# Squares summed by TensorE at a sublayer's end, additions to x on VectorE, low parts of the next weights on GpSimd

## Chip, cores and metric

One core of a Trainium2 chip runs the whole program. Its engines are PE (TensorE), DVE (VectorE), ACT (ScalarE), POOL (GpSimd) and SP (SyncE, which issues the DMAs). The metric is the time on the device of one execution in microseconds, as the median of several runs.

## The reference

The input is x (512 tokens of width 1024, fp32). A first block has a hybrid mixer, a memory cross attention and a SwiGLU FFN, each with a norm before and a norm after it. A second block has two layers of FFN, mixer and FFN, whose norms are modulated by vectors that come out of products of a condition `c` with 144 blocks of `w_ada`. What matters here is the form of the first block's sublayers and of the norm that follows:

```python
def rms_norm(x, g):
    xf = x.astype(jnp.float32)
    y = xf * lax.rsqrt(jnp.mean(xf * xf, axis=-1, keepdims=True) + RMS_EPS)
    return (y * g.astype(jnp.float32)).astype(x.dtype)
...
def swiglu(h, w_gate_up, w_down):
    g, u = jnp.split(h @ w_gate_up, 2, axis=-1)
    return (jax.nn.silu(g) * u) @ w_down
...
        y = swiglu(rms_norm(x, pre_ffn_g[l]), w_gate_up[l], w_down[l])
        x = x + rms_norm(y, post_ffn_g[l])
```

## The kernel before

x is kept transposed, as eight tiles X[m] of 128 features by 512 tokens (m = 0 to 7). Every large product runs as three products in a reduced fp32 format, on high and low parts of both factors. `weights()` loads a weight block of 128x1024 (`wr`), ACT makes its high part (`wh`, L338) and DVE, or an engine `e`, the low part, the rest of the subtraction (`wl`, L340). Three raw blocks, six high and six low parts can be alive.

PE runs in an order that a small planner (`Flow`) writes down ahead: every stream of work yields pieces with their cost on PE, or a wait whose length comes from a table of delays (`T`), and the order in which pieces come up is PE's order, kept as it is. The orders of DVE, ACT, POOL and SP are made by the language's scheduler, from the program and the dependences. Every engine works strictly in its order.

A sublayer's last product is taken in two halves of 256 tokens (`slab4`, products into `slh`). `end_post` handles the ends of the first block's three sublayers. For each m the slab's result is added to y on DVE (`evac`, L566), ACT squares y (L487) and POOL adds the squares up (`square_sum`, L490). When a half is through, a stream `norm(hf)` starts: PE sums the squares over features by products with ones (`ms`, L464, in `cols`), DVE makes 1/sqrt in twelve small steps (`rs_m`, `rs_y`, `rs_w`, `rs_a`, L447 to L455), and PE broadcasts the result over the partitions (`bc`, L476, in `spread`). Then for each m DVE scales y (L576) and x takes it up (L578; even m on DVE, odd m on POOL). In two of the three ends, those after the mixer and after cross attention (`apart` given), the high and low parts of the next products are made from x at once and the norm over x is applied later. The end of the FFN has no `apart`: squares of x are summed again on POOL, PE sums them over features, and a second broadcast comes before the next FFN's inputs `hh` and `hl` can be made (`norm_half`, L515 to L528). That FFN begins with five weight blocks at once (`dense_t` with `ahead` = 5, products `mm`), first all of one half of the tokens, then the other.

`ada()` loads a modulation block by DMA and reduces it on DVE (L795), one each time that `weights()` pulls it while `calm`; `modulated(n)` pulls what is missing for sublayer n.

## Time and profile before

| | us |
|---|---|
| median of 3 runs | 2888.01 |
| the runs | 2886.16 to 2888.03 |
| profiled execution | 2887.57 |
| its span | 2885.5 |
| PE busy | 2784.1 (96% of the span) |
| DVE busy | 1534.0 (53%) |
| ACT busy | 1027.6 (36%) |
| POOL busy | 383.5 (13%) |

The span reaches from the first to the last instruction of the profiled execution; about 2 us lie around it. PE's share is an average over the whole program. Where PE is not full is seen from its waits and from windows of the span. All times within the span are counted from its start. The end of the first FFN, the one end without `apart`, lies at 831 to 896 us; the ends after the mixer and after cross attention lie at about 312 to 370 and 450 to 510 us.

### The profile page before, as it was taken

The numbers are of one execution on the slowest core, as the hardware profiler recorded it, in microseconds if no ns is written. First come the engines' busy times: TensorE is split into PE (matmuls) and PEld (weight loads), VectorE is DVE, ScalarE is ACT, GpSimd is POOL, SyncE is SP. The second block draws the span as 40 slices with busy tenths as digits, with TensorE's granted clock in tenths as the row PEclk, the third lists the DMA queues.
The fourth block names the chain that finished last, engine by engine and source line by source line (L and its number), as shares of the span: only waits on it lengthen the run. The fifth ranks groups of instructions, "written<-read, shape, count | busy, mean of one in ns | idle before, by whom it ended". The sixth has DMA issues, their size and how long they took to land. (4 is left out here: it accounts for less than half of the span.)

```text
span 2885.5 us, 36900 instructions
## 1 busy us (share of the span) xinstructions
PE 2784.1 (96%) x14492; PEld 2355.3 (82%) x14492; DVE 1534.0 (53%) x2931; ACT 1027.6 (36%) x1725; POOL 383.5 (13%) x376
## 2 busy tenths in 40 slices
PE   8999998999989999998799999999999988999999
PEld 7888878888878888887588888888888875888888
DVE  6465666645456444466766454463333667643333
ACT  4355444323233222245543222342222535432221
POOL 3010303101032000024310000110000232200000
PEclk9999999999998999999999999999999997999999
DMA  5322322555433555431115555353332321133322
GB/s 164 121 69 88 103 88 74 168 160 169 148 114 123 160 169 161 139 116 54 52 52 162 156 174 159 112 173 110 102 95 88 95 62 34 52 98 93 102 90 71
DMA packets 94606, 326.07 MB, mean 113 GB/s; under 512 B 11232, under 2 KB 15584, under 8 KB 94432
## 3 DMA queue, kind: packets, MB, share of 16 engines
q1 hardware_dynamic: 94288, 323.53, 36.4%
q8 instruction: 114, 1.87, 0.3%
q14 instruction: 60, 0.49, 0.1%
q10 hardware_dynamic: 144, 0.18, 0.0%
HBM read 321.37 MB, written 2.10 MB: 112 GB/s over the span
## 5 line engine op out<-in xcount | busy, mean ns | idle before, releaser
L338 ACT ACTIVATE wh<-wr 128x1024 fp32r<-128x1024 f32 x456 | 482.3, 1060 | 1273.0 <-PE mm L347 494.8
L346 PE MATMUL mm<-hh,wh 128*128 128x512 f32 (+1 forms) x2344 | 856.9, 366 | 7.3 <-ACT fqk L1352 2.4
L348 PE MATMUL mm<-hh,wl 128*128 128x512 f32 (+1 forms) x2344 | 852.4, 364 | 3.0 <-DVE wl L340 3.0
L347 PE MATMUL mm<-hl,wh 128*128 128x512 f32 (+1 forms) x2344 | 852.9, 364 | 1.7 <-DVE hl L500 1.6
L340 DVE TENSOR_TENSOR wl<-wr,wh 128x1024 fp32r<-128x1024 f32 x440 | 541.8, 1233 | 343.1 <-ACT wh L338 341.2
L346 PEld LDWEIGHTS mm<-hh,wh 128*128 128x128 f32 x2344 | 448.4, 191 | 76.6 <-ACT fqk L1352 3.3
L348 PEld LDWEIGHTS mm<-hh,wl 128*128 128x128 f32 x2344 | 448.4, 191 | 71.2 <-DVE wl L340 3.6
L347 PEld LDWEIGHTS mm<-hl,wh 128*128 128x128 f32 x2344 | 448.2, 191 | 69.6 <-DVE hl L500 2.0
L795 DVE CUSTOM_DVE_ANT_0 ada<-ada,c 128x1024 f32<-128x1024 f32 x144 | 180.4, 1253 | 314.4 <-DMA ada<-in_w_ada_dram 314.2
L346 PE MATMUL dn<-uh,wh 128*128 128x512 f32 x720 | 280.1, 389 | 0.0
L347 PE MATMUL dn<-ul,wh 128*128 128x512 f32 x720 | 280.1, 389 | 0.0
L348 PE MATMUL dn<-uh,wl 128*128 128x512 f32 x720 | 280.1, 389 | 0.0
L490 POOL TENSOR_TENSOR acc<-sq,sq 128x256 f32<-128x256 f32 (+1 forms) x34 | 38.3, 1129 | 1377.2 <-ACT sq L487 1377.2
L633 DVE TENSOR_TENSOR sg<-mm,sg 128x512 f32<-128x512 f32 x110 | 75.9, 690 | 181.8 <-PE mm L348 177.4
L346 PE MATMUL mmt<-wh,hh 128*128 128x512 f32 x352 | 147.1, 418 | 12.1 <-ACT wh L338 8.2
L348 PEld LDWEIGHTS dn<-uh,wl 128*128 128x128 f32 x720 | 135.1, 188 | 28.1
L346 PEld LDWEIGHTS dn<-uh,wh 128*128 128x128 f32 x720 | 135.1, 188 | 28.1
L347 PEld LDWEIGHTS dn<-ul,wh 128*128 128x128 f32 x720 | 135.1, 188 | 28.0
L347 PE MATMUL mmt<-wl,hh 128*128 128x512 f32 x352 | 141.3, 402 | 0.5 <-DVE wl L340 0.5
L348 PE MATMUL mmt<-wh,hl 128*128 128x512 f32 x352 | 141.4, 402 | 0.0
L490 POOL TENSOR_TENSOR acc<-acc,sq 128x256 f32<-128x256 f32 (+1 forms) x140 | 122.5, 875 | 72.5 <-ACT sq L487 57.3
L669 DVE SCALAR_TENSOR_TENSOR X<-dn,gate,X 128x512 f32<-128x512 f32 x64 | 48.0, 750 | 155.6 <-PE dn L348 155.6
(322 smaller groups left out, 3611.1 us busy)
## 6 DMA issues: line engine op xcount, KB each, us to landing
wr<-in_f_gu_dram SPq DMA_DIRECT2D x176, 512.0 KB, 3.6
ada<-in_w_ada_dram SPq DMA_DIRECT2D x144, 512.0 KB, 4.2
wr<-in_f_dn_dram SPq DMA_DIRECT2D x88, 512.0 KB, 3.5
wr<-in_w_gu_dram SPq DMA_DIRECT2D x44, 512.0 KB, 3.6
wr<-in_w_in_dram SPq DMA_DIRECT2D x28, 512.0 KB, 3.5
wr<-in_m_t_dram SPq DMA_DIRECT2D x24, 512.0 KB, 3.5
wr<-in_w_dn_dram SPq DMA_DIRECT2D x22, 512.0 KB, 4.0
wr<-in_m_v_dram SPq DMA_DIRECT2D x16, 512.0 KB, 3.5
```

Source lines behind the costliest of these rows:

```text
L338: nc.scalar.activation(hi, raw, AF.Copy)
L340: (e or nc.vector).tensor_tensor(lo, raw, hi.bitcast(F32), op=OP.subtract)
L346: mm(ps, ah, bh, start=start, stop=False)
L347: mm(ps, ah, bl, start=False, stop=False)
L348: mm(ps, al, bh, start=False, stop=stop)
L490: nc.gpsimd.tensor_tensor(acc, accs.pop(), sq, op=OP.add)
L633: nc.vector.tensor_tensor(t, ps, t, op=OP.mult)
L669: self.nc.vector.scalar_tensor_tensor(self.X[m], ps, gate(m), self.X[m], op0=OP.mult, op1=OP.add)
L795: nc.vector.tensor_tensor_reduce(out=w, in0=w, in1=c, scale=1.0, scalar=0.0, op0=OP.mult, op1=OP.add, accum_out=ml[:, i:i + 1])
```

## The change

Four things change.

1. At all three ends of `end_post` only the squares of m = 0 to 5 are added up on POOL; those of m = 6 and 7 go to PE's sum as they are. A half's sum takes six products where the first half took two and the second four.
2. At the end without `apart`, the squares of x are not added up on POOL at all. Each goes to PE's sum as soon as the planner brings it up (`cols_of`), two products with one column each. The additions to x run on DVE except m = 1 and 4. The delay `squares` is gone.
3. In the FFN that follows this end, the five weight blocks taken at once get their low parts on POOL.
4. `ada` finishes a group in the step of its last block, and `modulated` remembers how far it is, so that it pulls no block more than it needs. 144 blocks remain; four of them (the 47th, 87th, 91st and 131st load) come later.

```diff
@@ weights
         if self.due >= 1.0:
             self.due -= 1.0
-            next(self.beside, None)
+            self.adas = next(self.beside, 6)
...
-    def dense_t(self, srcs, X, evac, ahead=0):
+    def dense_t(self, srcs, X, evac, ahead=0, e=None):
...
-            ws.append(self.weights(srcs[i]))
+            ws.append(self.weights(srcs[i], e))
...
+    def cols_of(self, tiles, scale, out):
+        ms, first = self.ps("x", "ms"), True
+        for sq in tiles:
+            if isinstance(sq, Wait):
+                yield sq
+                continue
+            for j in range(2):
+                self.nc.tensor.matmul(ms[:, j:j + 1], sq[:, j * 128:j * 128 + 128], self.ones1,
+                                      start=first, stop=True, skip_group_check=True)
+                first = False
+            yield 0.44
+        out.append(self.rsqrt(ms[:, :2], 2, scale, RMS_EPS))
+
-    def spread(self, accs, ncol, scale, out):
+    def spread(self, accs, ncol, scale, out, tiles=None):
         y = []
-        yield from self.cols(accs, ncol, scale, y)
+        yield from self.cols_of(tiles, scale, y) if tiles else self.cols(accs, ncol, scale, y)
...
@@ end_post
             nc.vector.tensor_tensor(y, ps, y, op=OP.add)
-            self.square_sum(sums, y, self.half, o == 0 or m % 4)
+            self.square_sum(sums, y, self.half, m < 6)
...
             yield from self.spread(accs, 2, 1.0 / D, bc)
-            for m in range(NK):
-                yield Wait(T["post"])
-                x, y = self.X[m][:, sl], Y[m][:, sl]
-                nc.vector.scalar_tensor_tensor(y, y, self.vec(gpost, m), bc[0], op0=OP.mult,
-                                               op1=OP.mult)
-                (nc.gpsimd if m % 2 else nc.vector).tensor_tensor(x, x, y, op=OP.add)
-                if apart:
-                    self.gain_half(hf, m, nxt[0], H)
-                else:
-                    self.square_sum(sums2, x, self.rot, m % 4)
+            def added():
+                for m in range(NK):
+                    yield Wait(T["post"])
+                    x, y = self.X[m][:, sl], Y[m][:, sl]
+                    nc.vector.scalar_tensor_tensor(y, y, self.vec(gpost, m), bc[0], op0=OP.mult,
+                                                   op1=OP.mult)
+                    e = nc.gpsimd if (m % 2 if apart else m in (1, 4)) else nc.vector
+                    e.tensor_tensor(x, x, y, op=OP.add)
+                    if apart:
+                        self.gain_half(hf, m, nxt[0], H)
+                    else:
+                        sq = self.half("sq")
+                        nc.scalar.activation(sq, x, AF.Square)
+                        yield sq
             if apart:
+                yield from added()
...
             else:
-                yield Wait(T["squares"])
-                bc = []
-                yield from self.spread(sums2, 2, 1.0 / D, bc)
-                yield from self.norm_half(hf, bc[0], nxt[0], nxt[1], H)
+                bc2 = []
+                yield from self.spread(None, 2, 1.0 / D, bc2, added())
+                yield from self.norm_half(hf, bc2[0], nxt[0], nxt[1], H)
...
@@ ada
-                    yield 3 * l + j
+                    if i % 24 < 23:
+                        yield 3 * l + j
...
+                yield 3 * l + j + 1
...
@@ modulated
-        while next(self.beside, 6) < n:
-            pass
+        while self.adas < n:
+            self.adas = next(self.beside, 6)
...
                 yield from self.ffn(I["f_gu"][2 * l + j // 2], I["f_dn"][2 * l + j // 2], H,
-                                    self.x_evac(g), end2)
+                                    self.x_evac(g), end2, self.nc.gpsimd if n == 3 else None)
```

The diff alone doesn't show where the scheduler and the planner put things. On PE, at the end of the first FFN, before: the rows from the end of the slab's second half (`slh`) to the first product of the next FFN (`mm`). `acc` are sums that POOL made, `sq` single squares, `rs_y` the end of an rsqrt chain.

```order
L348 MATMUL slh_7619<-uh_7265,wl_7310 128x256
L464 MATMUL ms_7694<-ones_78,acc_7540 128x1
L464 MATMUL ms_7694<-ones_78,acc_7645 128x1
L464 MATMUL ms_7694<-ones_78,acc_7540 128x1
L464 MATMUL ms_7694<-ones_78,acc_7645 128x1
L464 MATMUL ms_7714<-ones_78,acc_7609 128x1
L464 MATMUL ms_7714<-ones_78,acc_7692 128x1
L464 MATMUL ms_7714<-ones_78,acc_7609 128x1
L464 MATMUL ms_7714<-ones_78,acc_7692 128x1
L476 MATMUL bc_7734<-ident,rs_y_7700 128x128 x2
L476 MATMUL bc_7741<-ident,rs_y_7720 128x128 x2
L346 MATMUL mm_7653<-hh_7272,wh_7649 128x256
```

The same place after the change; ms_7552 is the sum over x for the first half, ms_7709 that over y for the second half, ms_7768 that over x for the second half, bc_7713 and bc_7761 the broadcasts of the first two.

```order
L478 MATMUL ms_7552<-ones_78,sq_7684 128x1 x2
L478 MATMUL ms_7552<-ones_78,sq_7690 128x1 x2
L464 MATMUL ms_7709<-ones_78,acc_7589 128x1
L464 MATMUL ms_7709<-ones_78,sq_7617 128x1
L464 MATMUL ms_7709<-ones_78,sq_7645 128x1
L491 MATMUL bc_7713<-ident,rs_y_7695 128x128 x2
L464 MATMUL ms_7709<-ones_78,acc_7589 128x1
L464 MATMUL ms_7709<-ones_78,sq_7617 128x1
L464 MATMUL ms_7709<-ones_78,sq_7645 128x1
L491 MATMUL bc_7761<-ident,rs_y_7724 128x128 x2
L478 MATMUL ms_7768<-ones_78,sq_7771 128x1 x2
L346 MATMUL mm_7653<-hh_7269,wh_7649 128x256
```

Before, two finished sums follow the slab, then both broadcasts and the products. After, the first half's sum over x ends with two single squares, and the second half's sum over y, its broadcast and its first square of x stand ahead of the first product. The other squares of x of the first half (m = 0 to 5) stand inside the slab, those of the second half inside the next products, about one after each six products.

On POOL, at the same place, before: from the last sums over y of the first half on. Between them stand the additions to x.

```order
L490 TENSOR_TENSOR acc_7452<-acc_7434,sq_7450 128x256
L490 TENSOR_TENSOR acc_7504<-sq_7468,sq_7502 128x256
L490 TENSOR_TENSOR acc_7522<-acc_7504,sq_7520 128x256
L490 TENSOR_TENSOR acc_7540<-acc_7522,sq_7538 128x256
L578 TENSOR_TENSOR X<-X,y_5752 128x256
L490 TENSOR_TENSOR acc_7579<-sq_7567,sq_7577 128x256
L490 TENSOR_TENSOR acc_7587<-sq_7559,sq_7585 128x256
L578 TENSOR_TENSOR X<-X,y_5827 128x256
L490 TENSOR_TENSOR acc_7597<-acc_7579,sq_7595 128x256
L490 TENSOR_TENSOR acc_7617<-acc_7587,sq_7615 128x256
L490 TENSOR_TENSOR acc_7609<-acc_7597,sq_7607 128x256
```

And after; `wl` are the low parts of the next FFN's weights, X with y_5752 and y_5866 the additions of m = 1 and 4.

```order
L505 TENSOR_TENSOR acc_7413<-acc_7395,sq_7411 128x256
L340 TENSOR_TENSOR wl_7665<-wr_7661,wh_7663 128x1024
L505 TENSOR_TENSOR acc_7501<-sq_7461,sq_7499 128x256
L505 TENSOR_TENSOR acc_7519<-acc_7501,sq_7517 128x256
L340 TENSOR_TENSOR wl_7672<-wr_7668,wh_7670 128x1024
L505 TENSOR_TENSOR acc_7537<-acc_7519,sq_7535 128x256
L505 TENSOR_TENSOR acc_7559<-acc_7537,sq_7557 128x256
L597 TENSOR_TENSOR X<-X,y_5752 128x256
L340 TENSOR_TENSOR wl_7679<-wr_7675,wh_7677 128x1024
L505 TENSOR_TENSOR acc_7589<-acc_7559,sq_7587 128x256
L597 TENSOR_TENSOR X<-X,y_5866 128x256
```

Sums over x are gone from POOL, two of four additions to x too, and three low parts stand between the sums over y and ahead of both additions.

On DVE, at the end after the mixer, before: the end of the rsqrt chain of the second half's sum over y (rs_y_3525) and what follows, the chain for the rows of the first half's x (rs_m_3582 on).

```order
L452 TENSOR_TENSOR rs_a_3527<-rs_w_3526,rs_y_3525 128x2
L453 SCALAR_TENSOR_TENSOR rs_y_3525<-rs_a_3527,rs_y_3525 128x2
L455 SCALAR_TENSOR_TENSOR rs_w_3526<-rs_a_3527,rs_w_3526 128x2
L452 TENSOR_TENSOR rs_a_3527<-rs_w_3526,rs_y_3525 128x2
L453 SCALAR_TENSOR_TENSOR rs_y_3525<-rs_a_3527,rs_y_3525 128x2
L576 SCALAR_TENSOR_TENSOR y_2921<-y_2921,V,bc_3572 128x256
L447 TENSOR_SCALAR rs_m_3582<-ms_3575 128x2
L578 TENSOR_TENSOR X<-X,y_2921 128x256
```

And after, where the second chain has the names rs_m_3569 to rs_w_3571.

```order
L452 TENSOR_TENSOR rs_a_3527<-rs_w_3526,rs_y_3525 128x2
L447 TENSOR_SCALAR rs_m_3569<-ms_3566 128x2
L453 SCALAR_TENSOR_TENSOR rs_y_3525<-rs_a_3527,rs_y_3525 128x2
L455 SCALAR_TENSOR_TENSOR rs_w_3526<-rs_a_3527,rs_w_3526 128x2
L448 TENSOR_SCALAR rs_y_3570<-rs_m_3569 128x2
L452 TENSOR_TENSOR rs_a_3527<-rs_w_3526,rs_y_3525 128x2
L450 SCALAR_TENSOR_TENSOR rs_w_3571<-rs_m_3569,rs_y_3570 128x2
L453 SCALAR_TENSOR_TENSOR rs_y_3525<-rs_a_3527,rs_y_3525 128x2
L455 SCALAR_TENSOR_TENSOR rs_w_3526<-rs_a_3527,rs_w_3526 128x2
L452 TENSOR_TENSOR rs_a_3572<-rs_w_3571,rs_y_3570 128x2
L452 TENSOR_TENSOR rs_a_3527<-rs_w_3526,rs_y_3525 128x2
L453 SCALAR_TENSOR_TENSOR rs_y_3570<-rs_a_3572,rs_y_3570 128x2
```

The chain for the rows begins before the other has ended, and the two run in turns.

## Rows read from the trace of the kernel before

**Rows 1.** Windows: length, busy PE, PEld, DVE, ACT, POOL, granted clock, DMA share, GB/s.
```profile
845.00:855.00 10.00, 9.53 (x81) 9.33 (x80) 8.72 (x26) 5.51 (x11) 4.61 (x5) 1.00 0.35 104
855.00:865.00 10.00, 3.16 (x22) 3.08 (x20) 5.28 (x12) 4.08 (x11) 9.28 (x12) 0.68 0.16 53
865.00:875.00 10.00, 5.38 (x21) 4.62 (x22) 9.37 (x38) 2.12 (x6) 3.45 (x5) 0.50 0.33 107
875.00:890.00 15.00, 12.64 (x79) 12.29 (x77) 11.71 (x32) 6.74 (x18) 8.56 (x11) 0.75 0.12 36
890.00:900.00 10.00, 10.00 (x86) 10.00 (x85) 3.22 (x8) 3.74 (x10) 3.23 (x4) 1.00 0.01 2
```
**Rows 2.** Timeline of PE, 844 to 890: start, length, line, tiles, wait before it.
```profile
845.92 0.50 PE L464 MATMUL ms<-ones,acc 128*128 128x1 f32 x4
...
850.95 0.71 PE L476 MATMUL bc<-ident,rs_y 128*128 128x128 f32 x4 [0.47 <-DVE rs_y L453]
...
856.17 0.28 PE L464 MATMUL ms<-ones,acc 128*128 128x1 f32 x2
863.29 1.86 PE L464 MATMUL ms<-ones,acc 128*128 128x1 f32 x8 [6.84 <-POOL acc L490]
...
869.21 2.07 PE L476 MATMUL bc<-ident,rs_y 128*128 128x128 f32 x8 [2.32 <-DVE rs_y L453]
873.17 0.58 PE L346 MATMUL mm<-hh,wh 128*128 128x256 f32 x1 [1.88 <-ACT hh L527]
...
881.41 0.83 PE L464 MATMUL ms<-ones,acc 128*128 128x1 f32 x6 [2.36 <-POOL acc L490]
...
885.79 0.34 PE L346 MATMUL mm<-hh,wh 128*128 128x256 f32 x1
```
**Rows 3.** PE's waits, 850 to 885: us in total, times, longest.
```profile
PE ms L464 <- POOL acc L490: 9.5, 3, 6.8
```
**Rows 4.** Timeline of DVE, the rsqrt chain behind the first half's sum.
```profile
846.46 0.16 DVE L447 TENSOR_SCALAR rs_m<-ms 128x2 f32<-128x2 f32 x1
...
848.23 0.70 DVE L452 TENSOR_TENSOR rs_a<-rs_w,rs_y 128x2 f32<-128x2 f32 x1
...
850.73 0.16 DVE L453 SCALAR_TENSOR_TENSOR rs_y<-rs_a,rs_y 128x2 f32<-128x2 f32 x1
```
**Rows 5.** Timelines of POOL and DVE in the second block's mixer, at 1333.
```profile
1333.33 2.35 POOL L340 TENSOR_TENSOR wl<-wr,wh 128x1024 fp32r<-128x1024 f32 x1 [4.51 <-ACT wh L338]
...
1333.16 0.17 DVE L452 TENSOR_TENSOR rs_a<-rs_w,rs_y 128x16 f32<-128x16 f32 x1
1333.37 2.34 DVE L453 SCALAR_TENSOR_TENSOR rs_y<-rs_a,rs_y 128x16 f32<-128x16 f32 x1
```
**Rows 6.** Groups by shape, whole span: busy us, mean ns, idle before.
```profile
L340 DVE TENSOR_TENSOR wl<-wr,wh 128x1024 fp32r<-128x1024 f32 x440 | 541.8, 1233 | 343.1 <-ACT wh L338 341.2
...
L490 POOL TENSOR_TENSOR acc<-acc,sq 128x256 f32<-128x256 f32 x136 | 116.7, 859 | 64.4 <-ACT sq L487 49.2 <-POOL acc L490 4.6 <-issue 3.2
L340 POOL TENSOR_TENSOR wl<-wr,wh 128x1024 fp32r<-128x1024 f32 x16 | 37.9, 2367 | 68.4 <-ACT wh L338 58.6 <-issue 9.7
L576 DVE SCALAR_TENSOR_TENSOR y<-y,V,bc 128x256 f32<-128x256 f32 x48 | 21.7, 472 | 1.8 <-PE bc L476 1.8
L578 DVE TENSOR_TENSOR X<-X,y 128x256 f32<-128x256 f32 x24 | 15.0, 625 | 0.0
```
**Rows 7.** Timeline of ACT, a high part that the changed POOL follows.
```profile
846.00 1.06 ACT L338 ACTIVATE wh<-wr 128x1024 fp32r<-128x1024 f32 x1 [0.38 <-PE slh L347]
```
**Rows 8.** Timeline of DVE, the modulation chunk in the second chain.
```profile
866.47 1.21 DVE L795 CUSTOM_DVE_ANT_0 ada<-ada,c 128x1024 f32<-128x1024 f32 x1
```
**Rows 9.** Timeline of PE, broadcasts after the mixer and after cross attention.
```profile
353.29 1.22 PE L476 MATMUL bc<-ident,rs_y 128*128 128x128 f32 x4 [4.56 <-DVE rs_y L453]
...
500.64 1.19 PE L476 MATMUL bc<-ident,rs_y 128*128 128x128 f32 x4 [2.96 <-DVE rs_y L453]
```
**Rows 10.** The page: DVE's busy tenths in 40 slices of 72 us.
```profile
DVE  6465666645456444466766454463333667643333
```

More of the change, by code (lines that the diff above doesn't have):

```diff
@@ L292, in __init__ @@
         self.flow = Flow()
-        self.beside, self.calm, self.due = iter(()), True, 0.0
+        self.beside, self.calm, self.due, self.adas = iter(()), True, 0.0, 0
     def nm(self, s):
@@ L612, in rows_wide, with ffn @@
         self.nc.scalar.copy(self.wide[:, hf * 256:hf * 256 + 256], bc[0])
-    def ffn(self, gu, dn, H, acc_evac, end):
+    def ffn(self, gu, dn, H, acc_evac, end, e=None):
         nc = self.nc
@@ L640, in ffn @@
         for s, (k0, n) in enumerate(SLABS):
-            yield from self.dense_t([gu[2 * k0 + i] for i in range(2 * n)], H, evac(k0), 0 if s else 5)
+            yield from self.dense_t([gu[2 * k0 + i] for i in range(2 * n)], H, evac(k0), 0 if s else 5,
+                                    e if s == 0 else None)
             if n == 4:
```

## The prediction

> **What bounds it now.** I read the windows first, to find the place where the change works, then TensorE's (PE's) timeline and waits there. Over the whole span PE is the bound; it is almost full, so only stretches where it isn't can pay. The end of the first FFN, the one sublayer end without `apart`, is such a stretch: between 855 and 875 us PE is busy for 8.5 of 20 us, at a granted clock that falls to 0.50 (1.2 of its two levels, 1.2 and 2.4 GHz), after a stretch in which it was busy for 3.2 of 10 us, and it is full again only after 885 [rows 1]. The reader is to see in PE's rows what it waits for [rows 2]: the last slab's products end at 856.2, then come the sum over y (863.29, after 6.84 us of waiting), the broadcast (869.21), the next FFN's first product (873.17), a third sum (881.41, after 2.36 us), and products at full clock from 885.79. The three waits for POOL's additions are 9.5 us [rows 3]. So 29.6 us pass from 856.2 to 885.8, in which 39 of the next products are issued, worth 4.7 us at full clock (86 in 10 us, [rows 1]). Some 25 us, 0.9% of the time, is the most that any change of this place can give back.
>
> **Step 1, squares of y (three sublayer ends).** The first half's sum goes from 2 products to 6 (12 records for 4), the second half's from 4 to 6. Four records took 0.50 us [rows 2], so about 0.1 us each, and 0.8 us more in all for the first half, 0.4 for the second. The two POOL additions that go (0.86 us each, [rows 6]) were hidden behind slab products in the first half. So here the sum of the first half and the rsqrt chain behind it start 0.7 us later: 847.2 in place of 846.46 [rows 4].
>
> **Step 2, the next weights' rests on POOL.** A rest takes 2.37 us on POOL and 1.23 us on DVE [rows 6]. Of the five, two are made before this stretch, beside a full PE, and three inside it. What counts is not POOL's time but what it does to DVE. While POOL computed such a rest at 1333.33 (2.35 us), a DVE step on 128x16 numbers that usually takes 0.17 us took 2.34 us and ended with it [rows 5]; at 848.23 a step of the rsqrt chain took 0.70 us [rows 4] beside a POOL addition. DVE's additions to x with both operands in SBUF take 0.63 us in the mean, while the scaling that reads `bc` from PSUM keeps to 0.47 [rows 6]. So I count: a DVE step with all its operands in SBUF that comes during a rest on POOL waits for its end.
>
> The Trainium skill, SBUF — State Buffer, section "SBUF: two separate sides", states this as a rule: a GpSimd operation and a VectorE operation with two SBUF inputs share a port pair, whichever starts first holds it for its whole length, and the other blocks. Rows 5 agree with it to 0.03 us. If POOL worked beside DVE without this, the first chain would end 0.4 us before it does now (one DVE rest of 1.23 us less, 0.8 us of products more); by the rule it ends a microsecond later. It speaks against this part of the change.
>
> Step by step, on the clock of the trace of before. ACT makes the high part at 846.00 to 847.06 [rows 7], POOL the rest at 847.1 to 849.5. The chain's second step, due at 847.4, waits until 849.5; the ten that remain need some 0.2 us each and one y addition between, to 852.0, where it ended at 850.9 [rows 4]. The broadcast comes at 852.0 in place of 850.95 [rows 2]: **+1.0 us**.
>
> **Step 3, squares of x straight to PE.** This takes away POOL's six additions per half and the waits of rows 3. But PE obeys a written order, and in it the eight sums now stand between the last slab's products, one after each six. A square that is late stops the slab itself. X's first addition is due at 853.5; POOL began its next rest at 853.1 and holds it to 855.5. Three scalings (0.4 us apart) and two POOL additions follow; X1, on POOL behind them, is done at 858.3, its square at 858.7. PE's second sum therefore stands at 858.7, two thirds through the slab, where today the slab has ended 2.5 us before. The next group of products ends at 859.3. Then ACT makes a high part (1.06 us) ahead of the squares of X2 and X3: sums at 861.2 and 862.2. POOL's last rest runs 860.5 to 862.9, then one sum of y and X4, to 864.3; DVE's X5 and X6 wait for gaps, to 864.3, and a modulation chunk (1.21 us, [rows 8]) stands ahead of y's last addition but one (y of m = 6), whose square stands ahead of X4's on ACT. So the fifth sum is at 867.3 and the slab ends at 868.8. A high part and three squares later the last sum is at 871.3; the rsqrt chain behind it has one chunk in its way, as today (866.47, [rows 8]), and ends at 874.6. **The second broadcast comes at 874.7 in place of 869.21, +5.5 us**, though no POOL sum stands before it.
>
> **Step 4, the second half's own chain.** In the new order PE's first product of the next FFN stands behind the second half's first broadcast and its first square of x. That chain's twelve steps are interleaved on DVE with six scalings for the first half (0.4 us) and three rests (0.5 to 0.95): 7 us, broadcast at 882.0; scaling, addition, square and sum 3 us more, first product at 885.2 in place of 873.17 [rows 2]. From there half clock for some 4.5 us, as today from 881.41 to 885.79 [rows 2], 21 products and three sums, then 18 more at full clock with three sums. The 39th product, done at 885.8 now, is done at about 893: **+7 us at this place**. The third wait of today (2.36 us) is inside this number, gone.
>
> **Step 5, the two `apart` ends.** Only step 1 is there, with a changed order: the rows' sum moves ahead of the second half's broadcast, and the two rsqrt chains run interleaved. The mixer's broadcast waits 4.56 us for its chain today, the wide one after cross attention 2.96 us [rows 9]. At the mixer the chain now waits for POOL's last sum of x and ends about 1.8 us later, but the rows' chain no longer lies among the second half's additions. Bounds: both waits gone, -7.5 us; each longer by twelve steps of 0.2 us, +4.8 us. I take **-1 us**, since one chain is later and one is earlier by the same count of steps.
>
> **Step 6, the modulation chunks.** The same 144 are loaded and reduced; four move to a later FFN, where DVE gets 4 x 1.25 us. DVE is busy only three tenths in the slices from 1948 us on [rows 10] and PE waits for none of it, so 0; were that cover gone, 5 us.
>
> **Sum.** 2887.57 us is the profiled execution (span 2885.5), 0.44 us under the median of the runs. Plus 7, minus 1: 2893.6, and 2894.0 beside the median of 2888.01.
>
> **Rivals.**
> *Faster: the squares keep up.* If POOL's rests fall into gaps and X's eight additions go through at the 0.63 us of their mean [rows 6] with 0.4 us of scaling, the last square is there by 859.5 and the chain by 862. The second half's chain then ends near 868, and the first product is at 870.5, with no wait at 881: 39 products are done by 880.5, 5.5 us earlier than now. With 2 us from the `apart` ends this is 2880.5 us. For it: rows 3 are real waits, and POOL is busy 9.3 of 10 us between 855 and 865 [rows 1] with sums that mostly go. Against it: the rests stand in POOL's order ahead of X1 and X4. It decides at the first rest: if X0 gets in before 853.1, the slab runs 2 us sooner.
> *No change: the rests hold DVE less.* If X0 and X5 pass ahead of the rests, and the chain at 847 too, the second broadcast is at 870.0, as today, and only the second half's chain ahead of the first product costs: +3.5 us, with the `apart` ends 2890.5 us.
> *Slower still.* The slab itself now stops and goes, and PE could fall to half clock at 853 and not get it back until 895, as after the waits at 869 [rows 1]: 40 products more at 0.12 us each extra, +5 us, with the full cost at the `apart` ends 2904 us.
>
> **How the numbers follow.** A measurement of this kernel can tell 0.2% (5.8 us) from no change. Forecast (+3 to +12 us) 0.45, no change 0.25, faster 0.25, slower still 0.05. The forecast's point lies just above the bound and half of its chance is under it, so: faster by over 0.2% 0.27, within 0.34, slower 0.39. Its own range is 2890 to 2900 us. To leave out 2 in 10, the range reaches past the faster rival, to 2877, and up to 2902.
>
> **What would show it.** Right, if PE's new sums wait for squares inside the slab (five waits of 1 to 3 us before 870 on this clock), if DVE's steps of 0.16 us stretch to over 1 us while POOL makes a rest, and if the first product of the next FFN waits for the second half's broadcast. Wrong, if the slab runs through without waits, if POOL's rests end before X's first addition, or if the time moved at the two `apart` ends. The prediction fails most easily in steps 3 and 4, where each engine's order passes the delay on to the next: one hold of 2.4 us more or fewer is a third of the sum.

## The result, and the profile after

| | us |
|---|---|
| median of 4 runs after | 2903.45 (2901.43 to 2908.63) |
| median of 4 runs before | 2887.9 (2886.16 to 2888.03) |
| ratio | 1.0058, interval 1.0041 to 1.0075 |
| profiled execution after, its span | 2904.05, 2902.2 |

The change is slower by 0.58%, and 1.45 us above the end of the predicted range. The direction and the place were right; the price of the place was not.

How the place is measured. In both kernels ACT makes the high parts of the same weight blocks in the same order. One of them begins at 846.00 before [rows 7], just ahead of the place, and another, the first behind it, at 904.72 in this timeline row of ACT of the kernel before (start, length, line, tiles, wait):

```profile
904.72 1.06 ACT L338 ACTIVATE wh<-wr 128x1024 fp32r<-128x1024 f32 x1 [10.90 <-PE mm L347]
```

The same two, in ACT's timeline of the changed kernel:

```profile
843.93 1.06 ACT L338 ACTIVATE wh<-wr 128x1024 fp32r<-128x1024 f32 x1 [0.44 <-PE slh L347]
...
921.49 1.06 ACT L338 ACTIVATE wh<-wr 128x1024 fp32r<-128x1024 f32 x1 [8.27 <-PE mm L347]
```

So the place, from the one to the other, took 58.72 us before and takes 77.56 now: **18.84 us more**, where the prediction had 7. Ahead of it the changed kernel has gained 2.07 us, where the prediction had 1. The two make 16.77 us; the profiled executions differ by 16.48 (2904.05 and 2887.57), so in this execution what lies behind the place is as long as before. In other executions it is up to 5.8 us longer or shorter, and so is what lies ahead by some 4 us; that is why the place is measured by itself. To put a time of the trace after on the clock of before, add 2.07.

By the rows of PE, here and in [rows 2], the 18.84 us are made up so: 8.83 up to the second broadcast, the one for the first half's x (869.21 before, 875.97 after), 7.26 from there to the next FFN's first product (873.17 and 887.19), since the second half's chain now stands ahead of it, and 2.75 behind it, where the kernel before had a wait and a stretch of half clock of its own.

The windows of the changed kernel (columns as in [rows 1], which they answer):

```profile
845.00:855.00 10.00, 6.57 (x50) 6.16 (x50) 8.93 (x20) 2.80 (x6) 7.79 (x7) 0.88 0.22 62
855.00:865.00 10.00, 8.49 (x37) 7.90 (x37) 7.88 (x13) 2.66 (x6) 4.95 (x4) 0.50 0.26 97
865.00:875.00 10.00, 7.14 (x31) 6.76 (x31) 3.73 (x14) 2.73 (x7) 0.00 (x0) 0.50 0.33 105
875.00:890.00 15.00, 7.16 (x31) 6.82 (x32) 12.38 (x42) 7.52 (x19) 4.42 (x6) 0.50 0.12 35
890.00:900.00 10.00, 10.00 (x50) 10.00 (x49) 0.73 (x2) 0.78 (x3) 0.00 (x0) 0.50 0.01 2
900.00:905.00 5.00, 5.00 (x28) 5.00 (x29) 1.60 (x11) 0.00 (x0) 0.00 (x0) 0.61 0.00 0
```

The row to look at is 890 to 900. PE is busy for the whole 10 us and waits for nothing, yet gets 50 records done, where the kernel before had 86 in the same window [rows 1]. All 86 were products with 256 columns; of the 50 only 30 are, and 20 belong to five pairs with one column. Two things show there: the granted clock is 0.50 (1.2 GHz), so that a product follows the last after 0.21 us and not 0.12, and a pair takes 0.85 us. The clock is at that level in every window from 855 to 900.

PE's timeline (start, length, line, tiles, wait before it; it answers [rows 2]; single products are left out but for the first of the next FFN):

```profile
849.75 0.71 PE L491 MATMUL bc<-ident,rs_y 128*128 128x128 f32 x4 [0.45 <-DVE rs_y L453]
...
854.15 1.01 PE L478 MATMUL ms<-ones,sq 128*128 128x1 f32 x4 [2.98 <-ACT sq L602]
...
859.76 1.01 PE L478 MATMUL ms<-ones,sq 128*128 128x1 f32 x4 [0.90 <-ACT sq L602]
...
865.50 1.01 PE L478 MATMUL ms<-ones,sq 128*128 128x1 f32 x4 [1.11 <-ACT sq L602]
...
871.05 1.87 PE L478 MATMUL ms<-ones,sq 128*128 128x1 f32 x8 [1.54 <-ACT sq L602]
...
875.97 1.22 PE L491 MATMUL bc<-ident,rs_y 128*128 128x128 f32 x4 [1.77 <-DVE rs_y L453]
...
883.19 1.19 PE L491 MATMUL bc<-ident,rs_y 128*128 128x128 f32 x4 [4.93 <-DVE rs_y L453]
886.32 1.01 PE L478 MATMUL ms<-ones,sq 128*128 128x1 f32 x4 [1.94 <-ACT sq L602]
887.19 0.56 PE L346 MATMUL mm<-hh,wh 128*128 128x256 f32 x1
...
888.62 0.85 PE L478 MATMUL ms<-ones,sq 128*128 128x1 f32 x4
...
899.29 0.85 PE L478 MATMUL ms<-ones,sq 128*128 128x1 f32 x4
...
901.42 0.85 PE L478 MATMUL ms<-ones,sq 128*128 128x1 f32 x4
```

The reader is to see two stretches. From 854 to 872 the sums over x of the first half stand between the slab's products, and PE stops at them four times. From 886 to 902 those of the second half stand between the next FFN's products, a pair after each six, every 2.13 us, and PE doesn't stop at all after the first.

PE's waits, 840 to 910 (us in total, times, longest; [rows 3]):

```profile
PE ms L478 <- ACT sq L602: 8.5, 5, 3.0
PE bc L491 <- DVE rs_y L453: 7.2, 3, 4.9
```

POOL's additions of squares, 9.5 us in [rows 3], are gone from the waits at this place. 8.5 us of waiting for single squares and 7.2 for rsqrt chains stand there instead.

The holds that step 2 counted on, in the timelines of POOL and of DVE:

```profile
845.06 2.40 POOL L340 TENSOR_TENSOR wl<-wr,wh 128x1024 fp32r<-128x1024 f32 x1 [5.02 <-ACT wh L338]
...
850.97 2.35 POOL L340 TENSOR_TENSOR wl<-wr,wh 128x1024 fp32r<-128x1024 f32 x1
```
```profile
845.28 0.16 DVE L447 TENSOR_SCALAR rs_m<-ms 128x2 f32<-128x2 f32 x1 [0.81 <-PE ms L464]
845.48 2.00 DVE L448 TENSOR_SCALAR rs_y<-rs_m 128x2 int32<-128x2 int32 x1
...
851.31 2.29 DVE L597 TENSOR_TENSOR X<-X,y 128x256 f32<-128x256 f32 x1
```

A step on 128x2 numbers takes 2.00 us and ends at 847.48, where POOL's low part ends at 847.46. X's first addition begins 0.34 us into the next low part and takes 2.29 us, to 853.60, 0.28 us behind the low part's end.

### The profile page after: what moved, and what is told of

The parts are those of the page before. It is cut to its first block, busy times and chain, and to the rows that moved or that the text cites. A ratio compares the mean times of both kernels' runs of the same rounds, so it can differ in the third digit from the quotient of the medians.

```text
span 2902.2 us, 37042 instructions
## 1 busy us (share of the span) xinstructions
PE 2805.5 (97%) x14576; PEld 2376.5 (82%) x14576; DVE 1532.0 (53%) x2930; ACT 1026.5 (35%) x1725; POOL 373.2 (13%) x356
## 5 line engine op out<-in xcount | busy, mean ns | idle before, releaser
L340 DVE TENSOR_TENSOR wl<-wr,wh 128x1024 fp32r<-128x1024 f32 x435 | 534.3, 1230 | 345.2 <-ACT wh L338 343.5
L505 POOL TENSOR_TENSOR acc<-sq,sq 128x256 f32<-128x256 f32 (+1 forms) x27 | 31.1, 1151 | 1368.4 <-ACT sq L502 1368.4
L346 PE MATMUL mmt<-wh,hh 128*128 128x512 f32 x352 | 147.7, 419 | 11.4 <-ACT wh L338 8.4
L505 POOL TENSOR_TENSOR acc<-acc,sq 128x256 f32<-128x256 f32 (+1 forms) x126 | 110.8, 879 | 69.3 <-ACT sq L502 58.3
```

The costliest lines, as they stand in the source:

```text
L340: (e or nc.vector).tensor_tensor(lo, raw, hi.bitcast(F32), op=OP.subtract)
L346: mm(ps, ah, bh, start=start, stop=False)
L505: nc.gpsimd.tensor_tensor(acc, accs.pop(), sq, op=OP.add)
```

## The experiments

**Theory.** The 18.84 us come from the places of the sums over x: a late square stops the slab's own products, and the pairs with one column between the next FFN's products keep PE at half clock, which makes everything there dearer. **Rival 1.** They come from the low parts on POOL, which hold DVE and so make squares and chains late. **Rival 2.** The half clock after 886 only follows from the long waits ahead of it, and the pairs have no part in it.

Each experiment is measured twice: by the runs, against runs of the kernel before on the same chip, and by its trace, as the time from the high part that stands at 846.00 before to the one at 904.72. The two starts are read from ACT's timeline of each run. Two kernels that leave the sums over x and the additions of this place as before (x7 and x11) have 58.72 and 60.19 us there against 58.72, so differences under about 1.5 us tell nothing. The place comes from one execution of each run, and that is not the median one: the traced executions of x9, x1 and x5 lie 9.5, 4.3 and 2.5 us above the medians of their runs, that of x13 lies 3.2 below.

"To first" is the part of the place up to the next FFN's first product, from the start of that product in PE's timeline. It is 27.17 us before and 43.26 in the changed kernel.

| run | median, before beside it | ratio (interval) | place, us | against before | to first, us |
|---|---|---|---|---|---|
| x6_change_again | 2905.87, 2889.33 | 1.0062 (1.0049 to 1.0075) | 77.81 | +19.1 | 43.27 |
| x1_lows_on_dve | 2902.93, 2891.11 | 1.0038 (1.0024 to 1.0053) | 76.72 | +18.0 | 41.75 |
| x8_late_half_together | 2898.3, 2889.33 | 1.0033 (1.0021 to 1.0045) | 70.15 | +11.4 | 40.10 |
| x2_gathered | 2893.49, 2891.11 | 1.0006 (0.9997 to 1.0015) | 65.02 | +6.3 | 36.00 |
| x9_early_half_together | 2890.36, 2889.33 | 1.0 (0.9987 to 1.0012) | 63.82 | +5.1 | 35.94 |
| x5_extra_columns | 2900.72, 2891.11 | 1.0035 (1.0022 to 1.0047) | 67.69 | +9.0 | 27.16 |
| x12_extra_wide | 2890.07, 2889.96 | 0.9999 (0.999 to 1.0008) | 61.54 | +2.8 | 27.75 |
| x4_only_y | 2891.04, 2891.11 | 1.0002 (0.9993 to 1.001) | 60.99 | +2.3 | 26.41 |
| x10_adds_on_dve | 2887.12, 2889.96 | 0.9992 (0.9984 to 1.0001) | 60.33 | +1.6 | 28.85 |
| x11_blocks_only | 2889.0, 2889.96 | 0.9998 (0.9989 to 1.0007) | 60.19 | +1.5 | 27.10 |
| x7_apart_only | 2889.89, 2889.33 | 1.0004 (0.9996 to 1.0013) | 58.72 | 0.0 | 27.18 |
| x13_together_late | 2879.54, 2889.96 | 0.9963 (0.9951 to 0.9976) | 53.10 | -5.6 | 22.53 |

**x6_change_again: the changed kernel as it is.**

> The changed kernel once more, beside the others of this call. All theories: 15 us over the kernel before on the same chip (ratio 1.004 to 1.007), half clock from about 852 to 903 us.

The place costs 19.1 us again, so the number to explain is stable. But this execution reaches it at 848.27, where the first one did at 843.93: what lies ahead of it varies more than the place (below, under what was not expected).

**x1_lows_on_dve: the change without the low parts on POOL** (rival 1).

```diff
-                                    self.x_evac(g), end2, self.nc.gpsimd if n == 3 else None)
+                                    self.x_evac(g), end2, None)
```

> The changed kernel with the low parts of the five weight blocks back on DVE, all else kept. Theory (a rest on POOL holds DVE and stands ahead of the additions of m = 1 and 4): the second broadcast and the first product of the next FFN come 3 to 4 us earlier, the half clock behind them lasts as long, about 2900 us, 3 to 4 under the changed kernel. Rival (the written order of PE alone costs the time): as the changed kernel, 2903, or a little more, since DVE has five rests of 1.23 us again.

PE's waits in this run, 840 to 910:

```profile
PE ms L478 <- ACT sq L602: 7.3, 5, 2.3
PE bc L491 <- DVE rs_y L453: 6.9, 3, 4.9
```

The same five and three waits as in the changed kernel, 1.2 and 0.3 us shorter, and the place costs 18.0 us. By this trace the low parts on POOL are worth about a microsecond in the place: the holds of 2.00 and 2.29 us are real, but without them DVE makes the low parts itself, at 1.23 us each [rows 6]. The first product comes 1.5 us sooner, not 3 to 4 as expected. The runs leave room for more: the medians are 11.8 us over before here and 15.6 and 16.5 in the changed kernel, and the intervals of the ratios overlap. Either way most of the loss stays without the low parts on POOL, so rival 1 falls as the main cause.

**x8, x9 and x2: the sums of one half, or of both, in one piece.** In x8 the second half's eight sums over x stand together behind their last square, in x9 the first half's, in x2 those of both (there with a longer delay in the planner). The low parts stay on POOL. The core of the edit, in `cols_of`, as x2 has it:

```diff
         for sq in tiles:
             if isinstance(sq, Wait):
                 yield sq
                 continue
+            got.append(sq)
+        yield Wait(8.0)
+        ms, first = self.ps("x", "ms"), True
+        for sq in got:
             for j in range(2):
                 self.nc.tensor.matmul(ms[:, j:j + 1], sq[:, j * 128:j * 128 + 128], self.ones1,
                                       start=first, stop=True, skip_group_check=True)
                 first = False
-            yield 0.44
+        yield 0.44 * len(got)
```

In x8 and x9 the same is done for one half, with this delay (0 leaves the half as in the change):

```diff
@@ x8
+                yield from self.spread(None, 2, 1.0 / D, bc2, (added(), (0, 2.0)[hf]))
@@ x9
+                yield from self.spread(None, 2, 1.0 / D, bc2, (added(), (1.0, 0)[hf]))
```

> The changed kernel, but the eight sums of x of a half stand together, behind the slab for the first half and behind 27 products of the next FFN for the second. Theory (one-column products between the others keep PE's clock at half, and squares inside the slab stop it): the slab runs through, the granted clock is 1.00 within 5 us of the first product as in the kernel before, 2889 to 2893 us. Rival (the clock stays low because of the long idle time ahead, whatever stands between the products): it comes back 16 us after the first product again, about 2899 us.

> The changed kernel, but the second half's eight sums of x stand together, 60 products into the next FFN; the first half's sums stay inside the slab. Theory (one-column products between the next FFN's products kept the clock at half): the first product comes 3 us earlier, since no square stands ahead of it, and the clock is at 1.00 some 5 us later, 6 us more; 9 us under the changed kernel, 6 over before. Rival (the clock stays low because the slab ahead went at half clock): only the 3 us, 12 over before.

> The changed kernel, but the first half's eight sums of x stand together behind the slab; the second half's stay near the front of the next FFN, six pairs ahead of its first product and two between. Theory (the slab's own stops and its half clock cost 3 to 4 us, the sums ahead of the first product the rest): the slab ends near 856, 4 us are saved, and the first product waits for the second half's squares, so 10 to 12 us over before. Rival (the stops in the slab are the whole loss): as before.

In x8, the late half's, the place costs 7.4 us less than in the changed kernel (70.15 against 77.56). The slab is still stopped there. 3.2 us are spared up to the first product, since no square of the second half stands ahead of it any more, as expected; the other 4.2 lie behind it. PE's row of that product, and the windows:

```profile
884.33 0.56 PE L346 MATMUL mm<-hh,wh 128*128 128x256 f32 x1
```

```profile
875.00:890.00 15.00, 8.81 (x50) 8.76 (x51) 12.38 (x45) 7.20 (x18) 4.45 (x6) 0.59 0.12 36
890.00:900.00 10.00, 10.00 (x80) 10.00 (x79) 2.65 (x14) 1.10 (x4) 0.00 (x0) 0.88 0.01 2
```

The same long waits stand ahead as in the changed kernel (4.9 us for the second chain), but with no pairs between the products the clock comes back before 890, and 80 records go through from 890 to 900 in place of 50. This speaks against rival 2 and for the theory's second part, at a price of about 4 us in the change itself. The 80 records are not all products: the eight sums, 32 records, stand at 892.97.

In x9, the early half's, the place costs 13.7 us less. Here the expectation missed: more came back than it allowed. PE's waits, 840 to 910:

```profile
PE ms L483 <- ACT sq L616: 3.7, 5, 1.8
PE ms L492 <- ACT sq L616: 3.4, 3, 1.4
PE bc L505 <- DVE rs_y L453: 1.7, 2, 1.3
```

Line 492 has the first half's sums in one piece, line 483 the second half's pairs. The slab goes through, and with it the next sums over y and the first broadcasts move forward: the wait of 4.9 us for a chain is gone with the four stops. But the edit moves more than the first half's sums. Of the second half's eight pairs six now stand ahead of the first product (one in the changed kernel), as its expectation says, and only two are left between products. PE's timeline:

```profile
883.25 1.01 PE L483 MATMUL ms<-ones,sq 128*128 128x1 f32 x4 [0.54 <-ACT sq L616]
884.13 0.56 PE L346 MATMUL mm<-hh,wh 128*128 128x256 f32 x1
...
885.55 0.85 PE L483 MATMUL ms<-ones,sq 128*128 128x1 f32 x4
...
887.69 0.85 PE L483 MATMUL ms<-ones,sq 128*128 128x1 f32 x4
```

So x9 does not measure the slab alone: 7.3 of its 13.7 us are saved up to the first product and 6.4 behind it, where two pairs stand in place of seven. How much of the loss is the slab's by itself no run shows; by the rows of the changed kernel, 8.83 us stand ahead of the second broadcast (above). The two savings (7.4 and 13.7) don't add up, since both count pairs that went: in x2, with both edits, the place costs 12.5 us less than in the change. There a new wait comes in, since the second half's additions now stand on DVE ahead of the first half's inputs to the next FFN; PE's longest wait, 840 to 910:

```profile
PE mm L346 <- ACT hh L546: 6.6, 1, 6.6
```

**x5_extra_columns and x12_extra_wide: the suspect by itself.** Both are the kernel before with eight extra pairs of products, the first ahead of the next FFN's first product and then one after each six products of the first half of tokens; nothing uses their results. In x5 a pair is two products with one column, with constant operands, so that nothing is waited for; in x12 it is two products with 256 columns, on the high parts that are there anyway.

```diff
+                    if hf == 0 and done % 2 == 0 and done < 2 * extra:
+                        col = col or self.ps("x", "ms")
+                        for j in range(2):
+                            self.nc.tensor.matmul(col[:, j:j + 1], self.ident, self.ones1,
+                                                  start=True, stop=True, skip_group_check=True)
+                        yield 0.44
+                    done += 1
```

In x12 the product's line is this:

```diff
+                            self.nc.tensor.matmul(col[:, :256], ws[0][0][:, :128], X[0][0][:, sl],
```

> The kernel before with eight pairs of one-column products by ones on a constant tile, whose sums nobody uses, written between the first half's products of the next FFN, one pair after each six, as the sums stand in the changed kernel. Theory (such products between the others keep the clock at half): the granted clock stays at 0.50 until the last pair, some 8 us longer than the 885.8 us of before, about 2895 us. Rival (they cost only themselves): clock back near 886 to 888, 8 times 0.43 us, about 2891 us.

> The control of the extra columns: the same eight pairs at the same places of the kernel before, but 256 columns wide, products of operands that are there, whose sums nobody uses. Theory (it is the one-column products that keep the clock at half): clock at 1.00 near 886 us as in the kernel before, and the pairs cost 8 times 0.24 to 0.43 us, 2 to 4 us over before. Rival (any extra products behind the wait do the same): half clock until the last pair, 9 us over before as with the columns.

Windows of x5, then of x12:

```profile
885.00:895.00 10.00, 10.00 (x49) 10.00 (x49) 5.87 (x23) 2.64 (x7) 1.55 (x3) 0.50 0.17 53
895.00:900.00 5.00, 5.00 (x31) 5.00 (x32) 1.73 (x5) 2.29 (x6) 2.28 (x3) 0.69 0.00 0
```
```profile
885.00:890.00 5.00, 5.00 (x40) 5.00 (x40) 3.72 (x17) 1.42 (x4) 0.00 (x0) 0.90 0.29 105
890.00:900.00 10.00, 10.00 (x86) 10.00 (x85) 3.00 (x8) 3.52 (x9) 3.23 (x4) 1.00 0.01 2
```

And PE's rows, in x5 the last pair with the product ahead of it, in x12 a pair and the product behind it:

```profile
894.13 0.41 PE L348 MATMUL mm<-hh,wl 128*128 128x256 f32 x1
894.35 0.85 PE L373 MATMUL ms<-ones,ident 128*128 128x1 f32 x4
```
```profile
885.78 0.49 PE L373 MATMUL ms<-hh,wh 128*128 128x256 f32 x2
886.12 0.28 PE L346 MATMUL mm<-hh,wh 128*128 128x256 f32 x1
```

With the one-column pairs PE is still at half clock at the last pair, at 894.35, and goes to full clock only behind it, busy all the time. With the wide pairs in the same places it is at full clock from 886, as before (885.79, [rows 2]), though they have 512 columns a pair and not two. The one costs 9.6 us in the runs and 9.0 in the place, all of it behind the first product; the other 0.1, which is nothing, and 2.8. So the one-column pairs keep the clock down without any wait (x5's last wait before them ends at 882.23); rival 2 falls. Not all of the 9.0 us is the clock: at 0.85 us a pair the seven behind the first product take some 6 us themselves, by an estimate from the rows, and the products' half clock the rest. What in the pairs does it isn't settled: besides the columns, the two kinds differ in format (x4 against x2 records for two products) and in length, and no run changed one alone.

**x7_apart_only, x4_only_y, x11_blocks_only, x10_adds_on_dve: the other parts, one by one, on the kernel before.** x7 has edit 1 at the two `apart` ends, x4 at all three, x11 edit 4 alone. x10 leaves the sums over y as before; it has, at the end without `apart`, the additions to x on DVE (but m = 1 and 4) and the last two squares of x taken to PE as they are, with POOL's sums of the other six kept. Their lines:

```diff
@@ x7
-            self.square_sum(sums, y, self.half, o == 0 or m % 4)
+            self.square_sum(sums, y, self.half, m < 6 if apart else o == 0 or m % 4)
@@ x4
-            self.square_sum(sums, y, self.half, o == 0 or m % 4)
+            self.square_sum(sums, y, self.half, m < 6)
@@ x10
-                (nc.gpsimd if m % 2 else nc.vector).tensor_tensor(x, x, y, op=OP.add)
+                e = nc.gpsimd if (m % 2 if apart else m in (1, 4)) else nc.vector
+                e.tensor_tensor(x, x, y, op=OP.add)
-                    self.square_sum(sums2, x, self.rot, m % 4)
+                    self.square_sum(sums2, x, self.rot, m % 4 and m < 6)
```

x11 has no other lines than those of edit 4, as they stand in the change.

> The kernel before with the first part of the change at the two ends with apart alone. Theory (their order and one addition less gained 2 to 3 us): 2.5 us under before, ratio 0.999, and the end of the first FFN as in the kernel before. Rival (the gain there is given back by what comes later): as before.

> The kernel before with the first part of the change alone: squares of y of m = 6 and 7 go to PE directly at all three ends. Theory (this part and the order that goes with it gave 2 to 3 us at the two ends with apart): 2886 us, 2 under before, of which the end of the first FFN takes 1 back. Rival (those ends gained from other parts, the modulation blocks that came later): 2888 us or more.

> The kernel before with the later modulation blocks alone. Theory (their DMAs and their DVE time are hidden in both places): as before, within 2 us. Rival (four chunks less near the first block's ends give 1.2 us of DVE each, or the later FFN pays them): 3 to 5 us to either side.

> The kernel before with a small piece of the change at the end of the first FFN: additions to x on DVE but for m = 1 and 4, and the squares of x of m = 6 and 7 straight to PE, behind POOL's sums of m = 0 to 3 and of 4 and 5. No sum between other products, no low part on POOL. Theory (POOL's row of additions sets the two sums; it gets some 3 us shorter, against 1.4 us for eight more records at half clock): 1 to 3 us under before. Rival (DVE's additions hold POOL as long as POOL's did): as before.

None of them differs from before by more than its interval allows. The gain of 2 to 3 us that was expected of edit 1 is not there. In x7's trace the high part of 846.00 begins at 842.41, 3.6 us sooner, but its median is 0.56 us above before's: a gain at the `apart` ends of one execution is not to be found in the medians. In x4 the end without `apart` costs 2.3 us. x10 has the additions to x on DVE and no single pairs spread among the slab's or the next products (its sums stand in one piece for each half), and its place costs 1.6 us, about as much as in x11, which leaves its sums and additions alone: it isn't the additions.

**x13_together_late: what the runs point to.** The change with edits 1 and 4 and the additions as they are, low parts on DVE, each half's sums over x in one piece (a delay of 1.0 us in the planner), and the second half's additions 4 us later, so that they don't stand ahead of the first half's inputs (x2's new wait).

```diff
+                if hf and not apart:
+                    yield Wait(4.0)
...
-                yield from self.spread(None, 2, 1.0 / D, bc2, added())
+                yield from self.spread(None, 2, 1.0 / D, bc2, (added(), (1.0, 1.0)[hf]))
```

> The changed kernel with all sums of x together (the first half's behind the slab, the second half's 66 products into the next FFN), the second half's additions 4 us later in the planner, and the low parts on DVE. Theory (with no sum between other products and nothing of the second half ahead of the first product, the POOL sums that went are a gain): slab to 856, first product near 870, clock back within 5 us, 2 to 5 us under before. Rival (32 records of one column in a row cost 7 us at half clock, as much as POOL's sums): as before or 2 us over.

PE's timeline of this run and, behind it, its windows:

```profile
853.03 2.87 PE L492 MATMUL ms<-ones,sq 128*128 128x1 f32 x24
857.35 1.14 PE L492 MATMUL ms<-ones,sq 128*128 128x1 f32 x8 [1.45 <-ACT sq L618]
...
862.31 2.08 PE L505 MATMUL bc<-ident,rs_y 128*128 128x128 f32 x8 [1.26 <-DVE rs_y L453]
864.72 0.58 PE L346 MATMUL mm<-hh,wh 128*128 128x256 f32 x1 [0.34 <-ACT hh L556]
...
874.59 3.63 PE L492 MATMUL ms<-ones,sq 128*128 128x1 f32 x32
```
```profile
865.00:875.00 10.00, 9.94 (x71) 9.65 (x71) 10.00 (x25) 6.76 (x18) 4.39 (x6) 0.83 0.01 3
875.00:890.00 15.00, 15.00 (x116) 15.00 (x117) 7.17 (x27) 5.40 (x13) 2.49 (x4) 0.89 0.09 35
```

The next FFN's first product comes at 864.72 in place of 873.17 [rows 2] (887.19 in the changed kernel), the waits are 1.5, 1.3 and 0.3 us, and the clock is back to 0.83 from 865 on. It is faster than before by 0.37% (0.24 to 0.49%), the only version here whose interval lies below before's time, and by more than the 2 to 5 us expected: 10.4 us between the medians, of which its trace shows 5.6 in the place. With the sums where x13 has them, that PE sums the squares of x itself is thus no loss. x13 differs from the change in three things. x1 has the low parts alone and x2 the sums' place (with a longer delay); the later additions were not tried by themselves, so what they give is not shown.

## Why the prediction was wrong

**The step that failed is step 4's clock term**: "From there half clock for some 4.5 us, as today from 881.41 to 885.79". The stretch was read off the kernel before, where three sums stand ahead and plain products follow. In the change a pair stands after each six products, and half clock lasts from the first product, at 887.19, past the last pair at 901.42. The 36 products and five pairs from 887.19 to 899.29 take 12.1 us; the prediction had 39 products and six sums in 7.8. The 39th, behind a sixth pair, is done at about 901.0, on the clock of before 903.1 in place of the predicted 893: 10.1 us late, 4.1 of them because it began late (below) and 6.0 from the clock and the pairs. An estimate from the rows parts these: 18 products at 0.21 us in place of 0.12 make 1.7 us, and six pairs at 0.85 us make 5.1, where the prediction left about 1.1 for all six (21 products at half clock fill its 4.5 us by themselves, 18 at full clock 2.2 of the other 3.3). So the term was too small twice: half clock lasted longer, and the sums had almost no price. x5 and x12 show that the pairs hold the clock down; x8 gives the price in the change itself, 4.2 us behind the first product.

**Step 3 was right that late squares stop the slab, and missed the clock.** Five waits of 1 to 3 us before 870 were called; on that clock there are three (2.98, 0.90 and 1.11 us), a fourth at 873.1 (1.54) and one in the second half's first sum (1.94). X's first addition was to be held until 855.5; it ends at 853.60 (855.67 on before's clock), and the first sum begins at 856.22. But once PE has stopped, the rest of the slab runs at 0.50, so a group of six products and a pair takes 2.3 us (854.15 to the next pair at 856.45, by the timeline), which the prediction counted at full clock. The second broadcast comes at 878.04 on before's clock in place of 874.7: +3.3 us, so that 8.83 us of the loss stand ahead of it where the prediction had 5.5.

**Step 4's order was right.** The first product waits for the second half's chain, broadcast and first square; it comes at 889.26 on before's clock (885.2 predicted), 4.1 us late, 3.3 of them inherited.

**Steps 1 and 2 were right, to 0.2 us.** The sum behind y: rsqrt begins at 845.28, 847.35 on before's clock (847.2 predicted). The chain's second step is held until the low part's end, broadcast at 851.82 (852.0). The Trainium skill, SBUF — State Buffer, section "SBUF: two separate sides", has the shared port pair held by whichever starts first, the GpSimd operation or a VectorE operation with two SBUF inputs or in a two-port mode. The trace agrees for X's addition, which has two inputs (2.29 us, ended 0.28 us behind POOL's). The step of 2.00 us has one input only, so "two SBUF inputs", as the prediction has the rule, does not cover it, and whether it ran in a two-port mode no run here shows. The net price over the whole place is as small as step 2's own +1.0: x1's place is 0.8 us shorter than that of the first trace, since the low parts cost DVE 1.23 us each where POOL doesn't make them.

**Step 5 has the sign right in most traces and nothing in the runs.** In the changed kernel's timeline of PE the mixer's broadcast waits little, but the rows' sum now waits for POOL ([rows 9] has 4.56 us at that broadcast):

```profile
353.34 1.02 PE L464 MATMUL ms<-ones,acc 128*128 128x1 f32 x4 [2.25 <-POOL acc L505]
...
355.61 1.22 PE L491 MATMUL bc<-ident,rs_y 128*128 128x128 f32 x4 [0.41 <-DVE rs_y L453]
```

Of the 4.56 us 2.66 are left, most of them now at the rows' sum, behind POOL's last sum as the prediction said. The 2.07 us gained ahead of the place in this trace are a loss of 2.27 in x6's; x7's ratio of 1.0004 holds no gain or loss. **Step 6** was right: 0.9998 in x11.

**Rivals.** What came is the rival called slower still: half clock from 853, not got back until after 895 (903.77 in the trace after, 905.8 on before's clock), with its 5 us too small and its chance of 0.05 far too low. That its 2904 us lie so near the measured 2903.45 is luck: some 5 us of it were the full cost at the `apart` ends, which no run shows. The faster rival, that the squares keep up, was decided as the prediction said, at the first low part: X's first addition was held. Yet x13 comes to about its time (2879.54; the rival had 2880.5) with no square waited for inside the slab.

## What to carry to other kernels

In an engine that keeps a written order, a short instruction that depends on a late result holds everything behind it: put the sums in one piece behind their last input, not between products that could run. Where small products are to be spread among large ones, look at the granted clock of the stretch afterwards and not at the busy share, which was 10.00 of 10.00 us while 30 products went through in place of 86. Such a product has a price of its own too: a pair with one column took 0.85 us at half clock, four times a product with 256 columns. A recovery time read from one place ("some 4.5 us") belongs to the instructions that stood there; with others between them it doesn't carry over.

## What the runs showed of the hardware that was not expected

With one-column pairs between 256-column products the granted clock stayed at 0.50 from 890 to 900 in the changed kernel with PE busy throughout, and up to x5's last pair at 894.35; with 256-column pairs in the same places (x12) it didn't. The Trainium skill, TensorE: Matmul & The Clock Gate, section "Part 1: The HAM clock gate", ties the clock to how busy PE has been; by the profile's count of busy time x5 doesn't agree with it, since 10.00 of 10.00 us went by at 0.50.

In one piece, too, one-column sums can cost clock. Behind the 32 records at 874.59 in x13 PE went at half clock from 878.8 to 882.0, and behind those at 892.97 in x8 from 897.8 to 901.0, without a wait; the mean clocks of 0.89 and 0.88 in their last windows above hold this. In x2 no such fall follows the 32 records at 885.07.

How long a stretch at half clock lasts also differs between executions of one kernel. After cross attention PE waits 2.36 us for a low part in both profiled executions of the changed kernel (its next product begins at 480.01 and at 480.58). A window behind it, of the first execution and then of x6:

```profile
485.00:490.00 5.00, 4.77 (x40) 4.56 (x39) 3.48 (x17) 0.82 (x2) 2.15 (x3) 1.00 0.39 116
```
```profile
485.00:490.00 5.00, 5.00 (x24) 5.00 (x25) 3.52 (x11) 0.81 (x2) 2.71 (x4) 0.50 0.32 105
```

In this window x6 is at 0.50 and gets 24 records done, the first execution at 1.00 gets 40. In the first execution the clock fell at 480.7 by PE's rows and was back at 484.1, ahead of the 12 one-column records of the sum over y. In x6 it fell later, at 482.1, and these records (484.25 to 486.7) came in the middle of its half clock; that they lengthened it was not tried. At 846 the two executions are 4.3 us apart (843.93 and 848.27). x9's trace has 0.50 in that window as well and begins the place at 848.19; the other six traces with edit 1 have 1.00 there and begin it at 842.2 to 844.2. The five without edit 1 begin it at 844.8 to 846.9.
